# Six attention heads for all tokens at once and two by token halves, with the queries and keys of the two kept on chip between the halves

## The chip, the cores and the metric

The kernel runs on one core of one Trainium2 chip. The metric is the device time of one execution, in microseconds (us). A core has a matrix engine (TensorE, PE in the profile, with PEld for its weight loads), a vector engine (VectorE, DVE), an activation engine (ScalarE, ACT), GpSimd (POOL) and SyncE (SP). Here SP issues most DMAs and POOL issues a few; all of them work side by side and wait for each other only where a semaphore says so. Each engine takes its own instructions in a fixed order.

## The reference, cut to what matters

The model has an mLSTM layer and then a differential attention layer, each followed by a squared-ReLU MLP; 1024 tokens, width 1024. The change touches only the attention: 8 heads, each with two score maps of width 64 and values of width 128, causal, in query blocks of 128 tokens.

```python
for blk in range(S // Q_BLOCK):
    q0 = blk * Q_BLOCK
    kv_len = q0 + Q_BLOCK
    ...
    p1 = jax.nn.softmax(jnp.where(mask, s1, -jnp.inf), axis=-1)
    p2 = jax.nn.softmax(jnp.where(mask, s2, -jnp.inf), axis=-1)
    a = (p1 - lam * p2).astype(v.dtype)
    outs.append(jnp.einsum('bhqk,bhkv->bhqv', a, v[:, :, :kv_len]))
o = jnp.concatenate(outs, axis=2)
o = rms_norm(o, subln_g, SUBLN_EPS) * (1 - lam_init)
return o.transpose(0, 2, 1, 3).reshape(B, S, B_HEADS * B_V_DIM) @ w_out
```

## The kernel before, in words

Tokens are handled in two halves of 512. Queries (`qdr`), keys (`kdr`) and values (`vdr`) are written to DRAM by the projections and loaded head by head for the attention. A number is kept as a high and a low part, so a product of two such numbers is three matmuls (L189 to L191, and L265 to L267 for the value projection).

A **unit** is one head and one query block, (h, qb); it has n = qb + 1 key blocks. In the order of the program it consists of

- `scores` (L971): for each of the two maps f, matmuls of the query block with the keys' two parts `ka` and `kb` (L985, L986) and a diagonal mask (L987) into PSUM; DVE takes the maximum (L989, L991), ACT the exponential and its sum (L995). There are two PSUM buffers for this, so a map's matmuls wait until ACT has read the map before the last.
- `combine` (L999): DVE joins the two maps (L1006), PE transposes the result block by block (L1012), ACT copies it out (L1013).
- `values` (L1016): n products with the head's values `v` (L1026), a copy and a sum of squares on ACT (L1027, L1029).
- after four units of one head, `subnorm` (L1033): four transposes (L1041) and a scaling that gives the operands `yh` and `yl` of the output projection for that head and half. If the place in `yh` and `yl` is still read by the value projection, the result goes to DRAM through POOL (`odr`, L1051) and comes back later by `reload` (L1053, L1056, POOL too); otherwise it is written in place (`direct`, L1043 and L1044).

`load` (L950) fetches a head's queries and keys for the tokens of one job, `load_v` (L967) its values. Both allocate from a pool with two buffers for each name, so a load waits until the head before the last has been read. All their DMAs stand on SP's queue.

Two other pieces of PE work are laid between the units. `chunks` (L1058) is the rest of the value projection: 24 steps of 24 matmuls each, called **fills** here, numbers 4 to 24 within the loop (steps 1 to 3 are ahead of it). Fills 17 to 24 make the values of heads 6 and 7, token block by token block; every second fill stores to `vdr` through ACT and POOL (L902, L905). `project_a` (L1075) is the output projection for the first token half: 8 steps of 24 matmuls of 512 columns, which read the residual `xs` and a weight tile `w_do`. After the loop the same projection for the second half follows (`gemm` at L1172, the same lines L189 to L191).

The loop over the units (L1126) sets the order: in step i it emits the fills that are due, loads, the scores of unit i + 2, combine of unit i, a subnorm, values of unit i - 1, and from a certain point a step of `project_a`. `jobs` (L1099) lists the heads: the first `FULL` of them with all 8 query blocks, then the rest with blocks 0 to 3 and after that once more with blocks 4 to 7. `project_a` begins one step after the last head's subnorm of the first half.

```python
for j, (h, q0, q1) in enumerate(jobs[1:]):
    ln = jobs[j][2] - jobs[j][1]
    load_at[n + 1] = (h, q0, q1)
    v_at[n + ln - 2] = (h, q0, q1)
    if h >= 2 and due[-1][1] < (h // 2 - 1) * NC + q1:
        due.append((n + ln - 2, (h // 2 - 1) * NC + q1))
    n += ln
```

From what the loop emits a scheduler makes the final order of each engine when the program is built; that order is shown below where it matters.

Of the kernel before, what the change touches and what calls it, by code (L numbers as in the profile page):

```python
# [9 lines left out]
F32R = mybir.dt.float32r  # L10
# [7 lines left out]
P = 128  # L18
T = 1024
# [6 lines left out]
BH, BD, BV = 8, 64, 128  # L26
# [2 lines left out]
FFG = (FN,) * FG  # L29
PSEQ = ((0, 1), (0, 2), (0, 5), (0, 6), (1, 1), (0, 7), (1, 5), (0, 3), (1, 6), (0, 4), (1, 2), (2, 1), (1, 7), (2, 5),  # L30
        (1, 3), (2, 6), (1, 4), (2, 2), (3, 1), (2, 7), (3, 5), (2, 3), (3, 6), (2, 4), (3, 2), (3, 7), (3, 3), (3, 4))
AHEAD, LAG, FULL, FILL0 = 2, 2, 5, 3
CUT = 256
LSZ = (2, 2, 1, 3)
QKORD = (2, 3, 4, 5, 0, 1, 6, 7)
# [20 lines left out]
def tile_yoco(ctx: ExitStack, tc: tile.TileContext, x, c, pos, cst, vec, bg, lp, ada,  # L56
              w_in, w_v0, w_v, w_o, w_mo, w_kv, w_vb, w_q, w_do, w_up, w_dn, out):
    nc = tc.nc
    pe, act, dve, sp = nc.tensor, nc.scalar, nc.vector, nc.sync
# [15 lines left out]
    def f32(ap):  # L75
        return ap.bitcast(F32)
# [20 lines left out]
    kdr = dr.tile([2, 2 * BH, BD, T], F32, tag="kdr", name="kdr")  # L97
    qdr = dr.tile([2 * BH, 2, BD, T], F32, tag="qdr", name="qdr")
# [113 lines left out]
    def gemm(srcs, nk, ah, al, consume, nbg=1, halves=(0, 1), first=2, hooks=None,  # L212
# [6 lines left out]
        def load(g):  # L219
            return [srcs[i] if isinstance(srcs[i], tuple) else  # L220
                    wload(srcs[i], [P, nk, P], nbg, hpool=pool if i >= early else None) for i in g]

        nxt = load(groups[0])
        for gi, g in enumerate(groups):
            ws, n = nxt, len(g)
# [13 lines left out]
            for pi, cells in enumerate(passes):  # L239
                for c in cells:  # L240
                    held[c] = cut1(gps(), c[0])
                for k in range(nk):
                    for h, i in cells:
                        mm3(held[h, i], ws[i][0][:, k], ws[i][1][:, k], ah(h, k), al(h, k), k == 0, k == nk - 1)
                    if k == 0 and pi == 0 and gi + 1 < len(groups):
                        nxt = load(groups[gi + 1])
                for h in halves:
                    if joint == gi and (h, 0) in held and (h, 1) not in held:
                        continue
                    idx = sorted(i for hh, i in held if hh == h)  # L250
                    if idx:
                        consume(g[idx[0]], h, [held.pop((h, i)) for i in idx])
                        if after and idx[-1] == n - 1 and (gi, h) in after:
                            after[gi, h]()
# [185 lines left out]
    with ExitStack() as ph:  # L440
# [16 lines left out]
        def small(name):  # L457
            return mp.tile([P, NC, AH], F32, tag=name, name=name)
# [15 lines left out]
        m, fp, nb0, fe, ml, u, mm, b0, me, wsx, wold, em = [  # L474
            small(n) for n in ("m", "fp", "nb0", "fe", "ml", "u", "mm", "b0", "me", "wsx", "wold", "em")]
# [466 lines left out]
    with ExitStack() as ph:  # L942
        kp = ph.enter_context(tc.tile_pool(name="kp", bufs=2))
# [4 lines left out]
        heads, units, lead = {}, {}, [None]  # L948

        def load(h, b0, b1):  # L950
            ka, kb, qs = [], [], []
            qt, kt = slice(b0 * P, b1 * P), slice(0, b1 * P)
            for f in range(2):
                g = 2 * h + f
                a = kp.tile([P, T], F32R, tag=f"ka{f}", name="ka")
                b = kp.tile([P, T], F32R, tag=f"kb{f}", name="kb")
                q = kp.tile([P, T], F32R, tag=f"q{f}", name="q")
                sp.dma_start(out=f32(q[:, qt]), in_=qdr[g, :, :, qt].rearrange("s d t -> (s d) t"))
                for s, t in ((0, a), (1, b)):
                    for dup in range(2):  # L960
                        sp.dma_start(out=f32(t[dup * BD:dup * BD + BD, kt]), in_=kdr[s, g, :, kt])
                ka.append(a)
                kb.append(b)
                qs.append(q)
            heads[h] = dict(ka=ka, kb=kb, qs=qs)

        def load_v(h, b0, b1):  # L967
            heads[h]["v"] = kp.tile([P, NC, BV], F32, tag="v", name="v")
# [148 lines left out]
        norms, back, begun, ahead, steps = [], ([], []), [], [], []  # L1117
        fill, proj, done = chunks(), project_a(), FILL0
        load(*jobs[0])
        load_v(*jobs[0])  # L1120
        for _ in range(done):
# [4 lines left out]
        for i in range(len(seq) + 2 + LAG):  # L1126
# [20 lines left out]
            while norms and norms[0][0] < i - LAG:  # L1147
                h, half = norms[0][1:3]
# [6 lines left out]
            if 0 < i <= len(seq):  # L1155
                h, qb = seq[i - 1]
# [139 lines left out]
```

## Time and profile before

| what | value |
|---|---|
| time, median of 3 runs | 2408.21 us (2405.18 to 2410.25) |
| the profiled execution's own time | 2406.43 us |
| its span, first to last instruction | 2404.7 us |
| lowest of the three runs | 2405.18 us |
| DVE busy | 1555.4 us (65%) |
| ACT busy | 985.1 us (41%) |
| HBM read and written over the span | 110 GB/s |

Times inside the profile are counted from the start of the span. The attention stage lies between about 1324 and 1666 us. "Idle before" in a timeline row is how long that engine stood still ahead of the row, and what released it. The trace shows two matmuls for each value product of one block (576 for the 288 of the program), so a value product of 4 blocks shows as x8 there and as x4 in the order.

### The profile page before, as it was taken

What the parts mean: (1) busy time and instruction counts of PE and PEld (TensorE: products, weight loads), DVE (VectorE), ACT (ScalarE), POOL (GpSimd) and SP (SyncE); (2) the same over time, 40 slices, a digit from 0 to 9 for tenths busy, and PEclk for the clock granted to TensorE, in tenths of its full rate; (3) what the DMA queues carried; (4) which work ended last, traced back from release to release, by engine and by line L of the source; (5) the groups of instructions that cost most, each with busy time, mean ns of one, the idle gap of its engine ahead of it and who ended that gap; (6) DMA issues with size and microseconds to landing.
All of it is one profiled execution on the core that took longest, in us unless ns stands there. A gap on an engine that the chain in (4) does not pass through costs nothing.

```text
span 2404.7 us, 30832 instructions
## 1 busy us (share of the span) xinstructions
PE 2354.6 (98%) x12020; PEld 1977.5 (82%) x12020; DVE 1555.4 (65%) x2559; ACT 985.1 (41%) x1882; POOL 39.1 (2%) x76
## 2 busy tenths in 40 slices
PE   7999999999999999999999999999999999999997
PEld 4899998778888888878788899888878888888886
DVE  7426544787877777777563377675676567566666
ACT  4324633444234323424332477764433333432332
POOL 0000000000000000000000011110000000000000
PEclk9999999999999999999999999999999999999999
DMA  7312142313423432442644654674121111111122
GB/s 309 121 56 85 68 161 79 116 51 123 140 77 90 141 111 65 127 153 79 203 134 149 203 167 154 209 212 167 57 66 35 53 62 44 40 62 57 36 96 79
DMA packets 105757, 266.80 MB, mean 111 GB/s; under 512 B 11786, under 2 KB 43018, under 8 KB 103820
## 3 DMA queue, kind: packets, MB, share of 16 engines
q1 hardware_dynamic: 100876, 250.16, 32.1%
q0 software_dynamic: 4736, 14.68, 1.9%
q8 instruction: 94, 1.54, 0.3%
q14 instruction: 51, 0.42, 0.1%
HBM read 228.03 MB, written 36.77 MB: 110 GB/s over the span
## 4 chain that ended last, share of the span: by engine, by line
PE 80%; DMA 5%; DVE 2%; ACT 1%; issue 0%; SPq 0%; DVEq 0%; ACTq 0%
PE gps L189 23%; PE gps L191 23%; PE gps L190 23%; PE gps L1026 2%; PE gps L265 2%; PE gps L267 2%; PE gps L266 2%; PE sc L985 1%; PE sc L986 1%; PE tps L1012 1%; DMA kb<-kdr 1%; DMA wraw<-in_w_do_dram 1%; DMA ka<-kdr 1%; DMA wraw<-in_w_vb_dram 1%; DVE x L691 0%
## 5 line engine op out<-in xcount | busy, mean ns | idle before, releaser
L189 PE MATMUL gps<-yh,wh 128*128 128x512 f32 x1664 | 655.1, 398 | 4.6 <-DVE yl L1044 2.4
L190 PE MATMUL gps<-yl,wh 128*128 128x512 f32 x1664 | 657.8, 396 | 1.1 <-DVE yl L318 1.1
L191 PE MATMUL gps<-yh,wl 128*128 128x512 f32 x1664 | 655.1, 395 | 0.5 <-DVE wl L172 0.5
L189 PEld LDWEIGHTS gps<-yh,wh 128*128 128x128 f32 x1664 | 312.4, 188 | 82.9 <-DVE yl L1044 2.6
L190 PEld LDWEIGHTS gps<-yl,wh 128*128 128x128 f32 x1664 | 312.6, 188 | 77.2 <-issue 1.7
L191 PEld LDWEIGHTS gps<-yh,wl 128*128 128x128 f32 x1664 | 312.6, 188 | 77.1 <-DVE wl L172 0.9
L171 ACT CAST wh<-wraw 128x1024 fp32r<-128x1024 f32 (+1 forms) x152 | 159.3, 1049 | 407.0 <-DMA wraw<-in_w_up_dram 213.3
L691 DVE SCALAR_TENSOR_TENSOR x<-gps,mod,x 128x512 f32<-128x512 f32 x392 | 286.0, 745 | 48.5 <-PE gps L191 47.0
L172 DVE TENSOR_TENSOR wl<-wraw,wh 128x1024 fp32r<-128x1024 f32 (+1 forms) x152 | 185.9, 1223 | 181.6 <-ACT wh L171 133.9
L265 PE MATMUL gps<-wh,yh 128*128 128x256 f32 (+1 forms) x768 | 223.7, 291 | 5.0 <-ACT sv L902 3.6
L266 PE MATMUL gps<-wl,yh 128*128 128x256 f32 (+1 forms) x768 | 219.9, 286 | 0.0
L267 PE MATMUL gps<-wh,yl 128*128 128x256 f32 (+1 forms) x768 | 219.0, 285 | 0.0
L171 ACT CAST eh<-e 128x1024 fp32r<-128x1024 f32 x56 | 58.7, 1049 | 242.7 <-DVE e L672 242.7
L151 DVE CUSTOM_DVE_ANT_0 adar<-adar,sil 128x1024 f32<-128x1024 f32 x96 | 116.8, 1222 | 53.6 <-DMA adar<-in_ada_dram 52.9
L265 PEld LDWEIGHTS gps<-wh,yh 128*128 128x128 f32 x768 | 145.7, 190 | 6.8 <-ACT sv L902 3.9
L266 PEld LDWEIGHTS gps<-wl,yh 128*128 128x128 f32 x768 | 145.8, 190 | 1.0
L267 PEld LDWEIGHTS gps<-wh,yl 128*128 128x128 f32 x768 | 145.7, 190 | 0.7
L629 ACT ACTIVATE b<-gps 128x512 f32<-128x512 f32 x112 | 66.8, 597 | 177.3 <-PE gps L191 172.1
L995 ACT ACTIVATE pf<-sc,mx 128x256 f32<-128x256 f32 (+7 forms) x128 | 95.1, 749 | 18.7 <-DVE mx L989 12.1
L172 DVE TENSOR_TENSOR el<-e,eh 128x1024 fp32r<-128x1024 f32 x56 | 68.3, 1220 | 46.6 <-PE gps L190 44.4
L189 PE MATMUL gps<-th,lh 128*128 128x512 f32 x224 | 89.1, 398 | 0.5 <-DVE x L691 0.5
L191 PE MATMUL gps<-bh,el 128*128 128x512 f32 x224 | 88.3, 394 | 0.7 <-DVE el L172 0.7
(266 smaller groups left out, 3877.2 us busy)
## 6 DMA issues: line engine op xcount, KB each, us to landing
adar<-in_ada_dram SPq DMA_DIRECT2D x112, 512.0 KB, 4.2
wraw<-in_w_up_dram SPq DMA_DIRECT2D x72, 512.0 KB, 3.4
e<-in_w_dn_dram SPq DMA_DIRECT2D x56, 256.0 KB, 3.1
m<-in_w_dn_dram SPq DMA_DIRECT2D x56, 256.0 KB, 3.1
x<-in_x_dram SPq DMA_DIRECT2D x8, 1024.0 KB, 8.3
wraw<-in_w_mo_dram SPq DMA_DIRECT2D x16, 512.0 KB, 3.3
ka<-kdr SPq DMA_DIRECT2D x32, 256.0 KB, 8.9
kb<-kdr SPq DMA_DIRECT2D x32, 256.0 KB, 9.6
```

Of the source, the lines that this page charges most:

```text
L151: dve.tensor_tensor_reduce(r, r, sil, 1.0, 0.0, ALU.mult, ALU.add, mod[:, n:n + 1])
L171: act.copy(out=ph, in_=src)
L172: dve.tensor_tensor(out=pl, in0=src, in1=f32(ph), op=ALU.subtract)
L189: pe.matmul(ps, lhsT=wh, rhs=a, start=first, stop=False, skip_group_check=more)
L190: pe.matmul(ps, lhsT=wh, rhs=b, start=False, stop=False, skip_group_check=more)
L191: pe.matmul(ps, lhsT=wl, rhs=a, start=False, stop=last, skip_group_check=more)
L265: pe.matmul(ps, lhsT=a, rhs=wh[:, k % 4], start=k == 0, stop=False)
L266: pe.matmul(ps, lhsT=a, rhs=wl[:, k % 4], start=False, stop=False)
L267: pe.matmul(ps, lhsT=b, rhs=wh[:, k % 4], start=False, stop=k == NB - 1)
L629: act.activation(dst, ps, AF.Relu)
L691: dve.scalar_tensor_tensor(xs, ps, mcol(l, 5, nb), xs, ALU.mult, ALU.add)
L995: act.activation(pf[f][:, 0:n * P], pp[f][:, 0:n * P], AF.Exp, bias=mx[:, f:f + 1], accum_out=ls[:, f, qb % 4:qb % 4 + 1])
```

## The change

`FULL` goes from 5 to 6: heads 0 to 5 are done with all tokens in one go, heads 6 and 7 by halves. `load` no longer fetches a part for each half: at a head's first half it allocates the tiles for all tokens, fetches the first half's columns and behind them the second half's; at the second half it does nothing. The values are still loaded once for each half.

```diff
-AHEAD, LAG, FULL, FILL0 = 2, 2, 5, 3
+AHEAD, LAG, FULL, FILL0 = 2, 2, 6, 3
...
         def load(h, b0, b1):
-            ka, kb, qs = [], [], []
-            qt, kt = slice(b0 * P, b1 * P), slice(0, b1 * P)
-            for f in range(2):
-                g = 2 * h + f
-                a = kp.tile([P, T], F32R, tag=f"ka{f}", name="ka")
-                b = kp.tile([P, T], F32R, tag=f"kb{f}", name="kb")
-                q = kp.tile([P, T], F32R, tag=f"q{f}", name="q")
-                sp.dma_start(out=f32(q[:, qt]), in_=qdr[g, :, :, qt].rearrange("s d t -> (s d) t"))
-                for s, t in ((0, a), (1, b)):
-                    for dup in range(2):
-                        sp.dma_start(out=f32(t[dup * BD:dup * BD + BD, kt]), in_=kdr[s, g, :, kt])
-                ka.append(a)
-                kb.append(b)
-                qs.append(q)
-            heads[h] = dict(ka=ka, kb=kb, qs=qs)
+            if b0:
+                return
+            heads[h] = H = {key: [kp.tile([P, T], F32R, tag=f"{tag}{f}", name=tag) for f in range(2)]
+                            for key, tag in (("qs", "q"), ("ka", "ka"), ("kb", "kb"))}
+            for c0, c1 in ((0, b1 * P), (b1 * P, T)):
+                for f in range(2 if c1 > c0 else 0):
+                    g = 2 * h + f
+                    sp.dma_start(out=f32(H["qs"][f][:, c0:c1]),
+                                 in_=qdr[g, :, :, c0:c1].rearrange("s d t -> (s d) t"))
+                    for s, key in enumerate(("ka", "kb")):
+                        for dup in range(2):
+                            sp.dma_start(out=f32(H[key][f][dup * BD:dup * BD + BD, c0:c1]), in_=kdr[s, g, :, c0:c1])
```

In the changed file every line behind `load` stands 3 lines higher, so its L1023 is the L1026 of before. The order of all engines is the same up to about fill 17 and again from the second-half projection on. Three places differ in a way that the prediction speaks of.

**SP's queue, loads of a late head.** Before, the second load of head 5 (numbers of the key tiles: `ka_13434`, `kb_13435` for map 0, `ka_13442`, `kb_13443` for map 1), with the first-half values of heads 6 and 7 (`v_13098`, `v_13294`) in its midst:

```order
L961 DMA ka_13434<-kdr_81 64x1024
L958 DMA q_13436<-qdr_82 128x512
L969 DMA v_13098<-vdr_85 128x512
L961 DMA ka_13434<-kdr_81 64x1024
L961 DMA kb_13435<-kdr_81 64x1024
L969 DMA v_13294<-vdr_85 128x512
L961 DMA kb_13435<-kdr_81 64x1024
L958 DMA q_13444<-qdr_82 128x512
L961 DMA ka_13442<-kdr_81 64x1024 x2
L961 DMA kb_13443<-kdr_81 64x1024 x2
```

Now, the first-half load of head 7 (`ka_13462` and so on), with the first-half values of head 6 (`v_13289`) in its midst and the second half's columns of map 0 behind it:

```order
L962 DMA ka_13462<-kdr_81 64x512
L958 DMA q_13460<-qdr_82 128x512
L962 DMA ka_13462<-kdr_81 64x512
L962 DMA kb_13464<-kdr_81 64x512
L966 DMA v_13289<-vdr_85 128x512
L962 DMA kb_13464<-kdr_81 64x512
L958 DMA q_13461<-qdr_82 128x512
L962 DMA ka_13463<-kdr_81 64x512 x2
L962 DMA kb_13465<-kdr_81 64x512 x2
L958 DMA q_13460<-qdr_82 128x512
```

The full-width key loads that stood here are gone; half-width ones of the last head stand in their place.

**PE, the values of head 6, second half.** Its value tile is `v_13731` before and `v_13745` now; it holds what the last fill, number 24, has made. Before, its first use stands 86 rows behind the last matmul of fill 24:

```order
L189 MATMUL gps_13903<-yh_75,wh_13895 128x512
L190 MATMUL gps_13903<-yl_76,wh_13895 128x512
L191 MATMUL gps_13903<-yh_75,wl_13896 128x512
L1012 MATMUL tps_13977<-cs_70,pf_13798 128x128 x4
L985 MATMUL sc_13954<-ka_13640,q_13642 128x512
L986 MATMUL sc_13954<-kb_13641,q_13642 128x512
L985 MATMUL sc_13954<-ka_13640,q_13642 128x512
L986 MATMUL sc_13954<-kb_13641,q_13642 128x512
L987 MATMUL sc_13954<-negr_9122,identr_9121 128x128
L1012 MATMUL tps_13983<-cs_70,pf_13798 128x128 x2
L1026 MATMUL gps_13989<-v_13731,at_13873 128x128 x2
```

Now it stands 23 rows behind it. Ahead of the rows shown and behind fill 24 there are only 2 value products, the scores of one unit with 4 transposes between its maps, and 3 value products:

```order
L1038 MATMUL rps_13828<-cs_70,o32_13508 128x128 x4
L1009 MATMUL tps_13868<-cs_70,pf_13765 128x128 x4
L1023 MATMUL gps_13877<-v_13543,at_13810 128x128 x4
L1009 MATMUL tps_13874<-cs_70,pf_13765 128x128
L982 MATMUL sc_13845<-ka_13000,q_12998 128x512
L983 MATMUL sc_13845<-kb_13002,q_12998 128x512
L982 MATMUL sc_13845<-ka_13000,q_12998 128x384
L983 MATMUL sc_13845<-kb_13002,q_12998 128x384
L984 MATMUL sc_13845<-negr_9122,identr_9121 128x128
L1023 MATMUL gps_13923<-v_13745,at_13867 128x128 x4
```

The second half of head 5 and the first steps of `project_a`, which stood between, have moved: the former ahead of fill 24, the latter behind.

**PE, the end of the stage.** Before, the last subnorm's transposes (`rps_14556`) stand behind the last step of `project_a`, directly ahead of the second-half projection (`gps_14598`):

```order
L189 MATMUL gps_14515<-yh_75,wh_14437 128x512
L190 MATMUL gps_14515<-yl_76,wh_14437 128x512
L191 MATMUL gps_14515<-yh_75,wl_14438 128x512
L1041 MATMUL rps_14556<-cs_70,o32_14344 128x128 x4
L189 MATMUL gps_14598<-yh_75,wh_14588 128x512
L190 MATMUL gps_14598<-yl_76,wh_14588 128x512
L191 MATMUL gps_14598<-yh_75,wl_14589 128x512
```

Now (`rps_14500`) they stand ahead of the last two steps of `project_a` (`gps_14455` is the seventh of eight):

```order
L189 MATMUL gps_14419<-yh_75,wh_14397 128x512
L190 MATMUL gps_14419<-yl_76,wh_14397 128x512
L191 MATMUL gps_14419<-yh_75,wl_14398 128x512
L1038 MATMUL rps_14500<-cs_70,o32_14168 128x128 x4
L189 MATMUL gps_14455<-yh_75,wh_14435 128x512
L190 MATMUL gps_14455<-yl_76,wh_14435 128x512
L191 MATMUL gps_14455<-yh_75,wl_14436 128x512
```

So 48 matmuls of 512 columns lie between the last subnorm and the first use of its result.

The second-half subnorm of head 5 now comes while the value projection still reads its place, so it is no longer `direct`: one more pair of stores and one more pair of reloads stand on POOL's queue (12 reloads behind fill 24, where there were 10).

## The prediction

> **What bounds the kernel now.** I read the page first: TensorE is busy nearly throughout.
>
> ```profile
> span 2404.7 us, 30832 instructions
> PE 2354.6 (98%) x12020; PEld 1977.5 (82%) x12020; DVE 1555.4 (65%) x2559; ACT 985.1 (41%) x1882; POOL 39.1 (2%) x76
> ```
>
> The change adds and removes no matmul: it reorders those of the attention stage from about 1500 to 1666 us and fetches less. So it can only win what PE stands idle there, and what it runs at a lower clock. The busy time in stretches of 20 us (one of 40), second view, shows that (columns: length, PE, PEld, DVE, ACT, POOL, granted PE clock, DMA share, GB/s):
>
> ```profile
> 1480.00:1520.00 40.00, 40.00 (x316) 38.50 (x316) 30.34 (x64) 31.84 (x101) 4.31 (x8) 1.00 0.49 153
> 1540.00:1560.00 20.00, 17.61 (x139) 16.47 (x137) 11.19 (x32) 13.41 (x57) 3.31 (x7) 1.00 1.03 310
> 1560.00:1580.00 20.00, 17.83 (x119) 16.54 (x120) 15.16 (x26) 12.49 (x33) 3.58 (x7) 0.91 0.95 242
> 1580.00:1600.00 20.00, 20.00 (x136) 18.11 (x135) 15.79 (x26) 12.85 (x34) 2.91 (x6) 1.00 1.02 269
> 1600.00:1620.00 20.00, 18.82 (x105) 15.79 (x103) 11.10 (x19) 11.32 (x25) 0.00 (x0) 1.00 0.43 152
> 1660.00:1680.00 20.00, 17.61 (x77) 13.71 (x76) 6.74 (x9) 5.15 (x8) 0.00 (x0) 1.00 0.68 261
> ```
>
> PE is full up to 1540. Then 2.39 + 2.17 + 1.18 + 2.39 = 8.1 us are idle, and 0.09 x 20 = 1.8 us are lost to the clock: 9.9 us, 0.4% of the time, is the most that any reordering here can win. In the same stretch the DMA engines are full (share 0.95 to 1.03 from 1540 to 1600). The third view, PE's timeline, says what it waited for:
>
> ```profile
> 1544.79 0.46 PE L1026 MATMUL gps<-v,at 128*128 128x128 f32 x2 [1.51 <-DMA v<-vdr]
> 1554.48 0.47 PE L986 MATMUL sc<-kb,q 128*128 128x512 f32 x1 [0.45 <-DMA kb<-kdr]
> 1561.71 0.47 PE L986 MATMUL sc<-kb,q 128*128 128x512 f32 x1 [2.15 <-DMA kb<-kdr]
> 1607.83 0.50 PE L985 MATMUL sc<-ka,q 128*128 128x512 f32 x1 [0.54 <-ACT pf L995]
> 1611.39 0.49 PE L189 MATMUL gps<-yh,wh 128*128 128x512 f32 x1 [0.64 <-DVE xs L1089]
> 1666.34 0.50 PE L189 MATMUL gps<-yh,wh 128*128 128x512 f32 x1 [2.39 <-DVE yl L1044]
> 1666.68 0.39 PE L190 MATMUL gps<-yl,wh 128*128 128x512 f32 x1
> 1666.91 0.39 PE L191 MATMUL gps<-yh,wl 128*128 128x512 f32 x1
> ```
>
> In turn: head 6's first-half values; twice the second keys of head 5, loaded a second time; two short waits around `project_a`; and the last subnorm, directly ahead of the second-half projection, whose matmuls then start 0.23 us apart. Finer windows show the clock behind two of these waits:
>
> ```profile
> 1560.00:1564.00 4.00, 2.29 (x11) 2.27 (x12) 1.29 (x2) 0.00 (x0) 0.00 (x0) 0.76 1.05 274
> 1564.00:1568.00 4.00, 4.00 (x27) 3.71 (x25) 2.12 (x5) 3.31 (x9) 0.00 (x0) 0.81 1.03 227
> 1664.00:1668.00 4.00, 1.66 (x7) 1.39 (x8) 2.79 (x4) 1.47 (x3) 0.00 (x0) 1.00 1.02 398
> ```
>
> After the 2.15 us wait the clock lost 0.24 x 4 + 0.19 x 4 = 1.7 us; after the 2.39 us wait it lost nothing.
>
> **The change part by part.** *What goes.* Head 5 is loaded once, heads 6 and 7 no longer fetch their first keys again; the two key waits end with that: 0.45 + 2.15 + 1.7 = 4.3 us. The wait for head 6's first-half values goes too: behind fill 20, which makes them, now stand the scores of (5,7), a whole fill and the scores of three small units, more than the 9.3 us of PE work that lay there before (from the fill's end at 1533.97, quoted below, to the wait's begin at 1544.79 - 1.51): 1.5 us. At the end, 48 matmuls at 0.23 us, 11 us, now lie between the last subnorm and its use, so its 2.4 us go. Together 8.2 us. The two short waits (1.2 us) I leave in: ACT and DVE still prepare the weights there. If the work that now covers these places runs out, each returns at its own price.
>
> *What is new at head 7.* Its keys can be fetched only when the scores of (5,7) have freed the buffers, and until its first scores PE has 21 value blocks, 16 transposes, a subnorm, a fill and eight maps with 20 key blocks: by the durations worked out below 4.3 + 1.6 + 0.45 + 24 x 0.115 (half the columns of a 0.23 us matmul) + 20 x 0.14, about 12 us. In these SP's queue must bring 1.5 MB (eight transfers of 128 KB for the keys, two of 256 KB for the queries), beside the reloads of the first half on POOL's queue. Before, the second keys of head 5 came under the same reloads and were late by 0.45 and 2.15 us with 2.5 MB. Bounds: nothing, and all of the 4.3 us again. The smaller transfer is nearer to nothing: 0.8 us.
>
> *The wait that is added.* Head 6's second-half values hold what fill 24 makes. From a fill's last matmul the way is: ACT copies, POOL stores, SP waits for the store and issues the load, the load lands. Fill 20 and fill 24 show it (the DMA rows are the landing times of the transfers issued at 1537.21, at 1539.01 and at 1493.36, from the view of DMAs):
>
> ```profile
> 1533.69 0.28 PE L267 MATMUL gps<-wh,yl 128*128 128x256 f32 x1
> 1534.68 1.07 POOL L905 DMA_DIRECT2D vdr<-sv  x2 [5.19 <-ACT sv L902]
> 1537.21 0.37 SPq L969 DMA_DIRECT2D v<-vdr  x1
> v<-vdr SPq DMA_DIRECT2D x1, 256.0 KB, 7.4
> v<-vdr SPq DMA_DIRECT2D x1, 256.0 KB, 14.1
> v<-vdr SPq DMA_DIRECT2D x1, 512.0 KB, 4.2
> 1575.44 0.28 PE L267 MATMUL gps<-wh,yl 128*128 128x256 f32 x1
> 1576.42 1.07 POOL L905 DMA_DIRECT2D vdr<-sv  x2 [23.21 <-ACT sv L902]
> 1580.38 0.33 SPq L969 DMA_DIRECT2D v<-vdr  x1
> ```
>
> From the end of the fill to the load's issue it took 1537.21 - 1533.97 = 3.2 us and 1580.38 - 1575.72 = 4.7 us; I take 4.0. The landing took 4.2 us with quiet DMA engines, 7.4 and 14.1 us amid the reloads. In the new order two weight tiles (1 MB) stand ahead of it on SP's queue and 12 reloads run on POOL's, but no keys: 7.4, the middle row. So the values are there 11.4 us after fill 24 (7.4 to 18.8). What PE has to do until then, by start times:
>
> ```profile
> 1583.04 0.48 PE L985 MATMUL sc<-ka,q 128*128 128x512 f32 x1
> 1583.88 1.05 PE L1012 MATMUL tps<-cs,pf 128*128 128x128 f32 x8
> 1584.69 0.47 PE L985 MATMUL sc<-ka,q 128*128 128x512 f32 x1
> 1585.53 0.62 PE L1041 MATMUL rps<-cs,o 128*128 128x128 f32 x4
> 1585.98 1.06 PE L1026 MATMUL gps<-v,at 128*128 128x128 f32 x8
> 1586.80 0.48 PE L189 MATMUL gps<-yh,wh 128*128 128x512 f32 x1
> 1589.99 0.47 PE L985 MATMUL sc<-ka,q 128*128 128x512 f32 x1
> 1590.95 0.43 PE L1026 MATMUL gps<-v,at 128*128 128x128 f32 x2
> ```
>
> One map of 6 key blocks is 0.84 us, so 0.14 a block, one of 7 blocks 0.96, a transpose 0.10, a value block 0.82 / 4 = 0.205, a subnorm's transposes 0.45. The 23 rows hold 2 + 3 + 4 value blocks (1.85), two maps of 6 (1.68), one of 7 (0.96), 9 transposes (0.9) and one subnorm (0.45): 5.9 us. PE then waits 11.4 - 5.9 = 5.5 us (1.5 to 12.9). PE takes its rows in order, so all that is queued behind waits too: the second map of that unit, and with it DVE's maximum and ACT's exponential. A wait this long I charge the clock loss of the 2.15 us row, 1.7 us (0 to 1.7).
>
> The Trainium skill, TensorE: Matmul & The Clock Gate, Part 1, says that the clock falls to half after an idle window of about 3.4 us and rises after as long a busy one. By that the new wait costs half of 3.4 us, an estimate of 1.7 too, but the 2.15 us wait should not have lowered the clock, and the gain would be 1.7 us smaller; the row of 1560 to 1564 (0.76) speaks against it.
>
> *No fill behind it.* Between fill 24 and `project_a` stand the scores of five large units with no other PE work; before, a fill or a step of `project_a` stood between such units. The only such stretch of before is head 0's, where ACT and DVE set the pace:
>
> ```profile
> 1364.00:1368.00 4.00, 3.34 (x24) 2.80 (x23) 3.80 (x9) 4.00 (x15) 0.00 (x0) 1.00 0.02 4
> 1368.00:1372.00 4.00, 3.63 (x29) 3.32 (x28) 2.88 (x6) 3.61 (x12) 0.00 (x0) 1.00 0.00 0
> 1372.00:1376.00 4.00, 3.97 (x29) 3.56 (x28) 3.90 (x8) 3.57 (x12) 0.00 (x0) 1.00 0.00 0
> 1376.00:1380.00 4.00, 3.79 (x26) 3.25 (x25) 3.71 (x9) 3.52 (x9) 0.00 (x0) 1.00 0.48 147
> ```
>
> PE is idle 16 - 14.73 = 1.3 us in 16. The new stretch behind the wait has 18 value blocks, 21 transposes and six maps with 39 blocks, 3.7 + 2.1 + 5.5 = 11 us: 1.0 us (0, if ACT works ahead during the wait, to 2.0). Elsewhere the fills lie further apart but one still stands in every long unit pair: nothing, covered by PE's own work as from 1480 to 1520. The extra stores and reloads of head 5 on POOL are needed only by the second-half projection, about 90 us behind fill 24 (1575.72 to 1666.34): nothing.
>
> *The sum.* -8.2 + 0.8 + 5.5 + 1.7 + 1.0 = +0.8 us. Against the profiled execution's 2406.43 us that is 2407.2; that execution lies 1.8 us below the median of 2408.21, so on the scale of the medians I forecast 2409.0 us. With a landing of 5.5 to 9.5 us it is 2407 to 2411.
>
> **The rivals.** About 0.2%, 4.8 us, is what a measurement of this kernel can tell from no change.
>
> *Slower: the values come amid the reloads.* If the load lands as the one of 14.1 us did, the wait is 12.9 us, the sum +8.2, the time 2416.4. It decides from +4.8 on, a wait of 9.5 us, which is a landing of 9.5 + 5.9 - 4.0 = 11.4 us. For it: 12 reloads are issued within the same microseconds, as 10 were at 1536. Against: the keys that shared the engines then are absent. The Trainium skill, DMA: Bandwidth & Descriptors, Issuing engines are not separate DMA queues, says that DMAs of SP and POOL run on the same 16 engines and interleave; the 14.1 us row agrees.
>
> *Faster: the values come quickly.* With 3.2 + 4.2 us the wait is 1.5 us and, as after the 1.51 us wait, costs no clock; head 7's keys are in time, the two short waits (1.2 us) vanish. -8.2 - 1.2 + 1.5 + 1.0 = -6.9: 2401.3. For it: less is fetched, for each of the last three heads 3 MB of queries and keys instead of 1.5 + 2.5. Against: the reloads.
>
> *The saving is moved, not made.* Head 7's first keys wait as head 5's second did, 4.3 us instead of 0.8: +4.3, 2412.5. For it: same reloads, same distance. Against: 1.5 MB, not 2.5.
>
> **How the numbers follow.** Forecast 0.47, slower rival 0.20, faster rival 0.20, moved saving 0.13. Forecast and moved saving are within 0.2%: 0.60. The range reaches nearly to both outer cases: 2401.5 to 2415.5. All bounds at once (-8 and +13 us) lie outside it and count among the 2 in 10.
>
> **What would show it.** Right: no wait for `kb` of more than 1 us; none for `yl` ahead of the second-half projection; one PE row L1023 (`gps` from `v`) behind the last L267 with some 5.5 us idle, released by the DMA of `v`, and a granted clock of about 0.8 in the 4 us behind it. Wrong: that row without a wait, a wait of 10 us there, or idle time spread over L982 rows released by ACT, which would mean that the missing fills cost more than the values.

## The result, and the profile after

The changed kernel is slower. Its median is 2422.68 us (2420.33 to 2424.35, 6 runs) against 2407.07 us of before (2405.18 to 2410.25, 6 runs, the same chip): a ratio of 1.0064, 95% interval 1.0054 to 1.0075, or 15.6 us. The forecast was 2409.0 us in a range that ended at 2415.5. Its profiled execution took 2422.82 us. The page's head:

```profile
span 2421.1 us, 30800 instructions
PE 2362.9 (98%) x12020; PEld 1981.9 (82%) x12020; DVE 1556.3 (64%) x2559; ACT 987.9 (41%) x1882; POOL 41.4 (2%) x80
```

The matmuls are as many as before, yet PE is busy 8.3 us longer (2362.9 against 2354.6): at half clock the eight value rows at 1596.64 below are busy for 2.08 us, eight at full clock in the prediction for 1.06. Of these, 2.5 us lie ahead of the attention stage. The span grew by 16.4 us. The value projection's first matmul of the stage starts 1.7 us later (1325.30 us, before 1323.61), ahead of anything that the change moves; in the runs below it starts between 1322.78 and 1325.83. The other 14.7 us arise between there and the first microseconds of the second-half projection. PE's timeline of after names the waits (L1023 is the L1026 of before, L982 the L985, L1086 the L1089):

```profile
1325.30 0.28 PE L265 MATMUL gps<-wh,yh 128*128 128x256 f32 x1
...
1501.59 0.50 PE L982 MATMUL sc<-ka,q 128*128 128x512 f32 x1 [2.24 <-ACT pf L992]
1523.35 0.33 PE L982 MATMUL sc<-ka,q 128*128 128x128 f32 x1 [0.62 <-ACT pf L992]
1566.79 0.30 PE L982 MATMUL sc<-ka,q 128*128 128x128 f32 x1 [0.46 <-DMA ka<-kdr]
1567.95 0.30 PE L983 MATMUL sc<-kb,q 128*128 128x128 f32 x1 [0.86 <-DMA kb<-kdr]
1591.56 0.33 PE L1009 MATMUL tps<-cs,pf 128*128 128x128 f32 x1 [0.89 <-ACT at L1010]
1592.46 0.50 PE L982 MATMUL sc<-ka,q 128*128 128x512 f32 x1 [0.56 <-ACT pf L992]
1596.64 2.08 PE L1023 MATMUL gps<-v,at 128*128 128x128 f32 x8 [3.02 <-DMA v<-vdr]
1608.35 0.50 PE L982 MATMUL sc<-ka,q 128*128 128x512 f32 x1 [1.19 <-ACT pf L992]
1669.47 0.49 PE L189 MATMUL gps<-yh,wh 128*128 128x512 f32 x1 [1.09 <-DVE xs L1086]
1681.05 0.77 PE L189 MATMUL gps<-yh,wh 128*128 128x512 f32 x1 [5.72 <-DVE xs L1086]
```

These are 16.7 us of idle time where before had 7.7 in the six rows that the prediction shows. They lie, but for one row of 0.62 us, in five places: near 1500 (a unit's exponentials are late, 2.2 us), at 1567 (head 7's keys, 1.3), at 1592 to 1597 (head 6's second-half values and two short waits ahead of them, 4.5), at 1608 (units without a fill, 1.2), and at the end of the stage (6.8). The last row is the first matmul of the second-half projection; it waited for `project_a`'s eighth step, not for `yl`.

The clock is the other part. Stretches of after that are cut where the clock changes (the columns are those of the windows in the prediction: length, PE busy and so on, the granted clock is the third number from the end):

```profile
1499.98:1503.40 3.42, 1.63 (x10) 1.30 (x10) 1.67 (x4) 3.42 (x13) 0.54 (x1) 1.00 0.70 242
1503.40:1506.82 3.42, 3.42 (x14) 2.95 (x14) 2.84 (x7) 3.15 (x15) 0.54 (x1) 0.50 0.40 155
...
1592.15:1595.56 3.41, 1.16 (x5) 0.85 (x5) 2.07 (x5) 2.54 (x9) 2.03 (x4) 1.00 1.02 407
1595.56:1598.97 3.41, 2.33 (x10) 2.24 (x11) 0.36 (x1) 0.41 (x3) 0.55 (x1) 0.50 1.03 396
1598.97:1602.39 3.42, 3.42 (x12) 2.94 (x11) 1.16 (x2) 1.51 (x6) 0.00 (x0) 0.50 0.85 321
...
1674.06:1677.48 3.42, 1.27 (x6) 0.69 (x4) 1.21 (x2) 0.63 (x1) 0.00 (x0) 1.00 0.70 210
1677.48:1680.89 3.41, 0.00 (x0) 0.00 (x0) 1.89 (x2) 1.06 (x2) 0.00 (x0) 0.50 0.28 97
1680.89:1684.31 3.42, 3.26 (x8) 2.62 (x9) 0.69 (x1) 0.61 (x1) 0.00 (x0) 0.50 0.83 234
```

Half of the busy time in the rows at 0.50 is lost: 1.7 us behind the place at 1500, 1.2 + 1.7 = 2.9 behind the values, 1.6 at the end, 6.2 us in all against 1.7 before. Idle time and clock together: (16.7 - 7.7) + (6.2 - 1.7) = 13.5 of the 14.7 us. All idle time of PE between the two starts grew by 9.3 us (23.2 against 13.9), so most of the other 1.2 us is not in waits, and where it lies stays open.

Two places are not in the prediction. Near 1500 the releaser is ACT, so ACT's own timeline and SP's queue say why it was late:

```profile
1490.34 0.82 SPq L176 DMA_DIRECT2D wraw<-in_w_do_dram  x2
```

```profile
1499.36 1.04 ACT L171 CAST wh<-wraw 128x1024 fp32r<-128x1024 f32 x1 [3.44 <-DMA wraw<-in_w_do_dram]
1500.31 0.58 ACT L992 ACTIVATE pf<-sc,mx 128x384 f32<-128x384 f32 x1
```

The cast makes the weights of `project_a`'s second step, which are used more than 100 us later; the scheduler has put it here, ahead of a unit's exponentials. Its tile was asked for at 1490.34, behind ten key and query transfers of head 5 that are now full-width, and was there 9.0 us later. ACT stood still for 3.44 us and the exponentials with it. Before, the same cast waited 0.84 us and no PE row shows it.

The end of the stage is read from DVE's rows that finish a step of `project_a`, steps 5 to 8 (with the sum over step 7's square, L1093, among them), and from SP's queue:

```profile
1661.34 0.75 DVE L1086 SCALAR_TENSOR_TENSOR xs<-gps,mod,xs 128x512 f32<-128x512 f32 x1 [6.92 <-DMA xs<-xdr]
1668.67 0.74 DVE L1086 SCALAR_TENSOR_TENSOR xs<-gps,mod,xs 128x512 f32<-128x512 f32 x1
1673.83 0.74 DVE L1086 SCALAR_TENSOR_TENSOR xs<-gps,mod,xs 128x512 f32<-128x512 f32 x1
1675.32 0.69 DVE L1093 TENSOR_TENSOR acc<-acc,xq 128x512 f32<-128x512 f32 x1 [0.75 <-ACT xq L1092]
1680.04 0.75 DVE L1086 SCALAR_TENSOR_TENSOR xs<-gps,mod,xs 128x512 f32<-128x512 f32 x1
```

```profile
1651.23 0.92 SPq L337 DMA_DIRECT2D x<-xdr  x2
...
1676.04 0.32 SPq L1080 DMA_DIRECT2D xs<-xdr  x1
```

A step's 24 matmuls take 5.6 us. Step 8's were done at 1681.05 - 5.72 = 1675.33, but its residual tile was asked for only at 1676.04. `project_a` has two buffers for two kinds of tile, the residual `xs` and its square `xq`, which ACT makes and DVE adds up. Step 8's tile goes where step 7's square was, and the fetch was issued when the sum over that square had ended (1675.32 + 0.69 = 1676.01). The tile was added at 1680.04, and only that released the next projection. Step 5's tile was late as well: it came behind two transfers of 1 MB for the next projection.

### The profile page after: what moved, and what is told of

Same layout as the page of the kernel before. It is cut to its first block, busy times and chain, and to the rows that moved or that the text cites. A ratio compares the mean times of both kernels' runs of the same rounds, so it can differ in the third digit from the quotient of the medians.

```text
span 2421.1 us, 30800 instructions
## 1 busy us (share of the span) xinstructions
PE 2362.9 (98%) x12020; PEld 1981.9 (82%) x12020; DVE 1556.3 (64%) x2559; ACT 987.9 (41%) x1882; POOL 41.4 (2%) x80
## 4 chain that ended last, share of the span: by engine, by line
PE 80%; DMA 4%; DVE 2%; ACT 1%; issue 0%; SPq 0%; DVEq 0%; ACTq 0%
PE gps L189 23%; PE gps L191 23%; PE gps L190 23%; PE gps L1023 2%; PE gps L265 2%; PE gps L266 2%; PE gps L267 2%; PE sc L982 1%; PE sc L983 1%; PE tps L1009 1%; DMA wraw<-in_w_vb_dram 1%; DMA kb<-kdr 1%; DMA wraw<-in_w_do_dram 1%; DMA ka<-kdr 1%; DVE x L691 0%
## 5 line engine op out<-in xcount | busy, mean ns | idle before, releaser
L992 ACT ACTIVATE pf<-sc,mx 128x128 f32<-128x128 f32 (+7 forms) x128 | 95.2, 749 | 22.5 <-DVE mx L986 13.0
```

The costliest lines, as they stand in the source:

```text
L992: act.activation(pf[f][:, 0:n * P], pp[f][:, 0:n * P], AF.Exp, bias=mx[:, f:f + 1], accum_out=ls[:, f, qb % 4:qb % 4 + 1])
```

## The experiments

Theory A, as first put after the two traces: the loss is in the new order of the stage, at separate places. Rivals: B, the kept load itself; and, for each place, that the wait would only move. For the end of the stage the runs later needed two theories of their own, C (the 1 MB transfers) and D (the shared buffers). Each kernel ran in five rounds beside the kernel before; a difference in us is against the median of before from the same session (2405.74 us for runs 1 to 4, 2407.92 for 5 to 8, 2406.14 for 9 to 12) unless said otherwise.

**1. The change without its load.** `FULL` is 6, `load` is that of before.

```diff
-AHEAD, LAG, FULL, FILL0 = 2, 2, 5, 3
+AHEAD, LAG, FULL, FILL0 = 2, 2, 6, 3
```

> Six heads for all tokens and two by halves, but with the load of before: heads 6 and 7 fetch their first keys a second time, nothing is kept. Theory A: the loss of 15.6 us comes from the new order of the stage (the last three steps of project_a back to back, head 6's values behind a late last fill, a weight cast that blocks ACT behind a full-width key load) and not from the kept keys; then this kernel shows the same waits and takes 2420 to 2428 us, the change's time or a little more, since 2 x 2.5 MB are fetched where the change fetches 2 x 1.5 MB. Theory B: the kept load itself (40 half-width transfers issued in a row on SP's queue) costs most of it; then this kernel takes 2407 to 2412 us. PE waits of over 5 us ahead of the second-half projection speak for A.

Measured: 2428.24 us, ratio 1.0087 (1.0073 to 1.0101), 22.5 us slower than before. PE and ACT at the longest wait, and the end:

```profile
1602.97 0.79 PE L985 MATMUL sc<-ka,q 128*128 128x512 f32 x1 [9.82 <-ACT pf L995]
...
1687.21 0.76 PE L189 MATMUL gps<-yh,wh 128*128 128x512 f32 x1 [6.44 <-DVE xs L1089]
```

```profile
1600.49 1.04 ACT L171 CAST wh<-wraw 128x1024 fp32r<-128x1024 f32 x1 [8.52 <-DMA wraw<-in_w_do_dram]
```

B falls: without the kept keys the same order loses as much (by the medians more; the two intervals just touch). What the second fetch costs here is mostly a place in a queue: a weight tile stands behind the key transfers on SP's queue, and its cast blocks ACT for 8.52 us. The end waits as in the change.

**2. The last fills earlier.**

```diff
+        due[-1] = (due[-1][0] - 3, due[-1][1])
+
         def goal(i):
```

> The change with its last fills due three steps earlier, so that fill 24 stands 12 small score maps and two large ones ahead of head 6's second-half values. Theory A (the values wait is a matter of where fill 24 stands): the 3.02 us wait for v, the clock loss of 3.4 us between 1592 and 1604 and the two ACT waits ahead of it (0.89 and 0.56) go, some 1 to 2 us come back because five large units now have no fill between them: 2415 to 2419 us. Rival (the stretch is paced by ACT and DVE whatever the fills do): the idle time only moves to rows of the scores released by ACT, 2420 us or more. The wait of 5.72 us at the end of the stage stays in both.

Measured: 2413.08 us, ratio 1.0030 (1.0019 to 1.0041): 7.3 us slower than before where the change is 15.6 slower. PE's longest rows between 1570 and the end:

```profile
1582.66 0.71 PE L1023 MATMUL gps<-v,at 128*128 128x128 f32 x4 [1.27 <-ACT at L1010]
...
1672.02 0.76 PE L189 MATMUL gps<-yh,wh 128*128 128x512 f32 x1 [6.29 <-DVE xs L1086]
```

No row waits for `v` any more, no clock is lost there, and some 2.8 us in four rows released by ACT are what the stretch without fills costs. The gain of 8.3 us is a little more than A had it (4 to 8): the place's 4.5 + 2.9 us are gone, the keys' 1.3 with them, and the units without fills wait 1.6 us more than the 1.2 of the change, which makes 7.1. The idle time at the end is as it was.

**3. The weight casts late.** A list `exps` collects the exponentials of all units.

```diff
-            nxt = wload(None, [P, NB, P], 0, r=raws[0])
+            with tc.issue_after(exps[-6].ins):
+                nxt = wload(None, [P, NB, P], 0, r=raws[0])
...
-                        nxt = wload(None, [P, NB, P], 0, r=raws[nb + 1])
+                        with tc.issue_after(exps[-6].ins):
+                            nxt = wload(None, [P, NB, P], 0, r=raws[nb + 1])
```

> The change with the weight casts of project_a kept behind a unit's exponentials on ACT's queue that is emitted three units before the step. Theory A: the 3.44 us in which ACT stood still at 1499 for a weight tile, and with it PE's 2.24 us wait and 1.7 us of clock loss, go: 2418 to 2420 us. Rival (the exponentials were late by themselves, the cast only stood where ACT had nothing to do): the PE wait near 1500 stays and the time is 2421 us or more; also possible that project_a's first step then waits for its weights, which would show as a PE wait ahead of the first L189 of the stage.

Measured: 2415.92 us, but with runs from 2412.83 to 2421.40; ratio 1.0042 (1.0027 to 1.0056), which just touches the change's interval. The profiled execution is the longest of the six (span 2419.6). Near 1500 it shows:

```profile
1501.54 0.49 PE L1023 MATMUL gps<-v,at 128*128 128x128 f32 x2 [1.78 <-DMA v<-vdr]
```

The ACT wait is gone, so the cast did block ACT. Behind it stood a second wait: head 4's values, made by fill 16, come late too, and in this execution the clock was lost all the same. What the edit is worth alone, the spread leaves open.

**4. The steps in pairs.**

```diff
-                steps.append(next(proj, None))
+                for _ in range(2 if len(steps) in (1, 4) else 1):
+                    steps.append(next(proj, None))
```

> The change with project_a's second and third step, and its fifth and sixth, emitted in the same step of the loop, so that two of the eight steps are left behind the last values where there were three and a half. Theory A (steps that follow each other without other work are paced by the fetch of the residual and of the weights, about 6.2 us for 5.6 us of matmuls, and the projection behind has to wait for the last of them): of 1.09 + 5.72 us and 1.7 us of clock loss at the end some 2.4 to 3.5 us of idle time are left, as before the change: 2416 to 2419 us. Rival (the wait belongs to the handover between the two projections, wherever the steps stand): it stays at 5 us or more and the time at 2421 us or more.

Measured: 2419.87 us, ratio 1.0059 (1.0045 to 1.0073): not to be told from the change. PE's last wait, DVE's row for step 7, and SP's queue ahead of it:

```profile
1678.98 0.76 PE L189 MATMUL gps<-yh,wh 128*128 128x512 f32 x1 [5.70 <-issue]
```

```profile
1672.94 0.75 DVE L1086 SCALAR_TENSOR_TENSOR xs<-gps,mod,xs 128x512 f32<-128x512 f32 x1 [8.02 <-DMA xs<-xdr]
```

```profile
1661.73 1.40 SPq L337 DMA_DIRECT2D x<-xdr  x3
1663.17 0.75 SPq L1080 DMA_DIRECT2D xs<-xdr  x1
```

Step 8's sum with its residual tile ends 0.1 us ahead of PE's row (at 1678.88), so it is again what PE waited for. A's expectation fails: fewer steps at the end, the same wait. Here step 7's tile comes 9.8 us after its issue, behind 3 MB of `x`, and step 8's is asked for only at 1675.41, when the sum over step 7's square has ended. Hence theories C and D.

**5. The residual stream late** (C).

```diff
-        load_x(xt, xdr)
+        with tc.issue_after(xsd[0].ins):
+            load_x(xt, xdr)
```

`xsd[0]` is the last fetch of `xs`.

> The change with the load of the residual stream for the next projection (four transfers of 1 MB, three of which stood on SP's queue between the fetches of project_a's fifth to seventh step) kept behind project_a's last residual fetch. Theory C (formed after the paired steps moved nothing: 3 MB of that load delay the residual tile of step 5 to 8.6 us, and the steps behind never catch up, so the projection waits for step 8): the 5.72 + 1.09 us and 1.7 us of clock loss shrink to 1.5 to 3 us, 2416 to 2418 us. Rival D (two buffers shared by residual tile and its square: each fetch waits for the store of the step before, 6.2 us for 5.6 us of matmuls): the wait stays at 4 us or more and the time at 2421 us or more. A third case would be that the next projection now waits for the residual stream: a PE wait 5 to 15 us behind its start.

Measured: 2421.89 us, ratio 1.0050 (1.0037 to 1.0062), 14.0 us slower than before, not to be told from the change. DVE's rows for steps 5 to 8 and PE's last wait:

```profile
1661.24 0.75 DVE L1086 SCALAR_TENSOR_TENSOR xs<-gps,mod,xs 128x512 f32<-128x512 f32 x1 [2.36 <-PE gps L191]
...
1667.74 0.75 DVE L1086 SCALAR_TENSOR_TENSOR xs<-gps,mod,xs 128x512 f32<-128x512 f32 x1 [3.82 <-DMA xs<-xdr]
...
1673.91 0.75 DVE L1086 SCALAR_TENSOR_TENSOR xs<-gps,mod,xs 128x512 f32<-128x512 f32 x1 [3.69 <-DMA xs<-xdr]
...
1681.25 0.75 DVE L1086 SCALAR_TENSOR_TENSOR xs<-gps,mod,xs 128x512 f32<-128x512 f32 x1 [4.20 <-DMA xs<-xdr]
```

```profile
1682.11 0.76 PE L189 MATMUL gps<-yh,wh 128*128 128x512 f32 x1 [3.67 <-issue]
```

Step 5 is now in time, and from there a step takes 6.5, 6.2 and 7.3 us (the last beside the stream), each waiting for its tile: the shared buffers alone are slower than 5.6 us of matmuls. Here steps 6 and 8 waited for the store of the step before, step 7 for the sum over a square. C explains why step 5 was late, not the pace. It has a share in the end's wait all the same, which fell from 6.8 to 3.7 us, a little below the 4 us that D had set. The time did not follow in the profiled execution because head 7's keys cost 1.3 us of idle time and 3.0 us of clock more there than in the change.

**6. A ring of its own for the residual tile** (D). The two buffers `sv` are free once the fills are done.

```diff
-                xs = ap_.tile([P, HT], F32, tag="ot", name="xs", bufs=2)
+                xs = ap_.tile([P, 2, 2, BV], F32, tag="sv", name="xs").rearrange("p a b v -> p (a b v)")
```

> The change with project_a's residual tile in buffers of its own (the two that the fills' stores no longer use), so that a fetch no longer waits for the square of the step before; the load of the next projection's residual stream stays where it is, but step 5's tile is now fetched ahead of it. Rival D (the shared two buffers set the pace): the wait of 5.72 us goes, 2415 to 2418 us. Theory C (the 3 MB set it): step 6's tile now comes behind them, so the end improves by 3 us at most, 2419 to 2422 us.

Measured: 2415.07 us (11 runs), ratio 1.0028 (1.0018 to 1.0038): 8.4 us of the 15.6 are gone. DVE's row for step 8 and PE's last wait:

```profile
1670.06 0.75 DVE L1086 SCALAR_TENSOR_TENSOR xs<-gps,mod,xs 128x512 f32<-128x512 f32 x1 [0.38 <-PE gps L191]
```

```profile
1670.91 0.47 PE L189 MATMUL gps<-yh,wh 128*128 128x512 f32 x1 [0.89 <-issue]
```

The last step is now released by its own matmuls. D holds: with the 1 MB transfers still on the queue, the end's waits shrink from 6.8 to 0.9 us and no clock is lost there. A tile can now be asked for earlier: step 5's is issued at 1642.40, ahead of the 1 MB transfers (from 1647.27), where in the change it stood behind two of them. So the ring is enough to take the loss away; with it, the same transfers delay nothing that PE waits for.

**7 and 8. Three edits together, on the change and on before.** The fills three steps earlier ahead of all the heads that need them, the casts of run 3, the stream of run 5.

```diff
-                due.append((n + ln - 2, (h // 2 - 1) * NC + q1))
+                due.append((n + ln - 5, (h // 2 - 1) * NC + q1))
```

> The change with the fills due three steps earlier in front of heads 2, 4 and 6 alike, the weight casts of project_a late, and the residual stream late. If the causes are separate their gains add up: 9.6 for the fills, 2 to 4 for the cast and the values of head 4, 4 to 6 for the end: 2403 to 2407 us, level with before or faster. If they are one and the same slack that moves (DVE and ACT pace the units without fills), less than 12 us come: 2410 us or more.

> The kernel before (five heads at once, three by halves, keys fetched twice) with the same three edits as the kernel sent with it. Its residual stream was late already, and its values wait was 1.5 us, so there is less to repair: 1 to 4 us, 2403 to 2407 us. If head 6 in one go and the kept keys are worth what they removed (two key waits of 4.3 us with the clock loss), this kernel is 3 to 5 us slower than the changed one with the same edits; if it is faster, the split of three heads covers more than the kept keys save.

Measured: the change with them 2402.87 us, ratio 0.9975 (0.9964 to 0.9985), faster than before; its one long wait left is 3.61 us at the end. Before with them 2409.90 us, ratio 1.0006 (0.9996 to 1.0015). That misses the 2403 to 2407 us expected. The comparison of the two is not clean, since on before the late cast meets the second fetch of the keys; ACT and PE there:

```profile
1597.02 1.04 ACT L171 CAST wh<-wraw 128x1024 fp32r<-128x1024 f32 x1 [12.32 <-DMA wraw<-in_w_do_dram]
```

```profile
1600.40 1.11 PE L1012 MATMUL tps<-cs,pf 128*128 128x128 f32 x4 [8.05 <-ACT at L1013]
```

**9 and 10. Fills and ring, with and without the late casts.** Both have the fills of run 7 and the ring of run 6; the first also the casts of run 3.

> The change with the fills due three steps earlier ahead of heads 2, 4 and 6, the weight casts late, and the residual tile in its own ring in place of the late residual stream. From the kernel with the first two and the stream late (2402.9 us), whose last wait of 3.61 us and 1.7 us of clock loss belong to the shared ring if that sets the pace of back-to-back steps: 2397 to 2400 us. If the two repairs of the end are worth the same here: 2402 to 2404 us.

> The same without the late casts: the casts of the first two weight tiles stand again far ahead on ACT's queue. If a cast that waits for its tile behind a full-width key load blocks ACT (the 2.24 to 2.79 us waits near 1500 with the clock loss behind them), this takes 3 to 5 us more than its sister; if the earlier fills have already taken that wait away (the tiles are fetched earlier too), the same within 1 us.

Measured: with the casts 2398.15 us, ratio 0.9967 (0.9955 to 0.9980), 8.0 us faster than before; without 2401.83 us, ratio 0.9980 (0.9971 to 0.9988), 4.3 us faster. The two longest waits that the first has left from 1380 us on:

```profile
1589.26 0.50 PE L982 MATMUL sc<-ka,q 128*128 128x512 f32 x1 [0.81 <-ACT pf L992]
...
1658.94 0.47 PE L189 MATMUL gps<-yh,wh 128*128 128x512 f32 x1 [1.14 <-issue]
```

Its clock stays full from 1380 us through the stage. In the kernel without the late casts no row near 1500 waits longer than 0.5 us either: the earlier fills had fetched the weight tiles earlier too. Why it is 3.7 us slower is then open; its idle rows add up to only 0.7 us more, and the two intervals overlap.

**11. The ring on the kernel before.**

> The kernel before with the residual tile in its own ring and nothing else. There the steps of project_a stand between units, 7 to 10 us apart, so a ring of 6.2 us a step binds nothing: 2406 to 2408 us, within 0.1% of before, against 7.6 us that the same edit brought to the changed kernel. A gain of over 3 us would mean that the ring costs something by itself.

Measured: 2406.40 us, ratio 1.0002 (0.9993 to 1.0010). The last wait is the old one:

```profile
1666.67 0.50 PE L189 MATMUL gps<-yh,wh 128*128 128x512 f32 x1 [2.39 <-DVE yl L1044]
```

The ring is worth nothing where the steps end 7.5 us or more apart, and 8.4 us where the last ones touch. So it was the change that made it a bound.

**12. The second fetch of the keys, all else repaired.** Run 9 with the load of before.

> Six heads at once with the load of before (keys fetched twice) and with earlier fills, late casts and the ring. The distance to the sister with the kept keys is what keeping the keys is worth once nothing else waits: 5 us if its price in the unrepaired pair (2428.2 against 2422.7 us) was its own, 0 to 2 us if the second fetch of the keys hurt only because the values came late behind it.

Measured: 2402.91 us, ratio 0.9990 (0.9981 to 0.9999), 4.8 us more than run 9. Its PE rows that run 9 lacks:

```profile
1585.69 1.35 PE L1026 MATMUL gps<-v,at 128*128 128x128 f32 x10 [1.67 <-DMA v<-vdr]
...
1595.77 0.47 PE L986 MATMUL sc<-kb,q 128*128 128x512 f32 x1 [1.48 <-DMA kb<-kdr]
```

With 1.7 us for one stretch of 3.41 us at half clock behind the second they make 4.85 us: keeping the keys is worth its 4.8 us, once nothing else hides it. The other 3.2 us of run 9's gain are the new order with its repairs. Before was not run with all three of these repairs; those that it was run with (runs 8 and 11) made it no faster.

## Why the prediction was wrong, step by step

*The key waits and the first-half values go* (4.3 + 1.5 us): right. No row waits over 1 us for `kb`, none for head 6's first-half values.

*"At the end, 48 matmuls at 0.23 us, 11 us, now lie between the last subnorm and its use, so its 2.4 us go."* This is the step that failed. The wait for `yl` did go, but the cover was taken as free: the 48 matmuls were counted as work that flows at 0.23 us each, and their own supply was not asked for. Before, every step but the last had value products or scores beside it; now the last four follow each other with only a subnorm's four transposes between, and they are fed through two buffers that also take the square. Where a wait of 2.4 us stood there are 6.8 us of waits and 1.6 us of clock; that the buffers are what makes them is shown by runs 6 and 11. This term alone turns +0.8 into 9.2.

*"Elsewhere ... nothing, covered by PE's own work as from 1480 to 1520."* The second miss, and it lies in that very stretch. The fills were looked at, not the loads. A load is also a length: head 5's now has all tokens at once, a weight tile queues behind it, and ACT behind the tile's cast: 2.2 us and 1.7 us of clock. That the cast blocks ACT, run 3 shows; that the full width of the load makes it late is read from the trace, not tried alone.

*The values wait, 5.5 us and 1.7 of clock:* right in place and in mechanism, with some luck in the sum. The load was issued 4.4 us after the fill's end (taken as 4.0) and landed in about 6.5 (7.4); 3.02 us of wait for the values follow two short ones of 1.45 that ACT released and that the term did not have, and the clock, forecast at about 0.8 over 4 us, stood at 0.50 over 6.8 and lost 2.9. That is 7.4 us against 7.2: a shorter wait and a larger loss of clock offset each other. Run 2, which moved the fill, took away 8.3 us. The slower rival, a landing amid the reloads, did not happen.

*Head 7's keys, 0.8 us; the stretch without fills, 1.0:* measured 1.3 and 1.2.

*The two short waits left in, 1.2 us:* gone; one row of 0.6 us stands in another place.

The sum with what was measured: -8.2 + 1.3 + 7.4 + 1.2 + 3.9 + 8.4 - 0.6 = +13.4 us. So the sums of the terms that the prediction had were right within a microsecond, and the two that it put at a gain or at nothing are 12.3 us. Of the rivals the slower one came nearest in number (2416.4 us), by a landing that did not happen; a saving that is moved is what happened, but it went to `project_a`'s residual tile and not to head 7's keys.

## What to carry to other kernels

Work that is moved to cover a wait needs its own supply: before counting matmuls as cover, ask how long a step takes when its neighbour is another such step, which here is freeing a shared buffer (by a store or by the sum over a square), fetch and add: 6.2 to 7.3 us in run 5, for 5.6 us of matmuls. An instruction that prepares something for much later, and stands in an in-order queue ahead of something urgent, is harmless only while its input is early; a longer load elsewhere can end that. A sound change can lose to what it uncovers: with the fills earlier, the casts later and a ring for the tile, the same edit is 0.33% faster than before, and its own saving of 4.8 us shows.

## What the runs showed of the hardware

The prediction could not say why a wait of 2.15 us had cost clock and one of 2.39 had not. In the attention stage of every run the stretches at half clock last 3.41 us or two or three times that, and within a run they begin at multiples of 3.41 us from each other, so within a run there is a fixed raster. Cut along it, before shows:

```profile
1558.77:1562.19 3.42, 1.27 (x7) 0.79 (x7) 0.49 (x3) 0.76 (x5) 0.00 (x0) 0.99 1.07 229
1562.19:1565.60 3.41, 3.41 (x16) 3.23 (x16) 1.59 (x3) 1.51 (x6) 0.00 (x0) 0.51 1.03 274
...
1664.60:1668.01 3.41, 1.67 (x7) 1.40 (x8) 2.28 (x3) 0.87 (x2) 0.00 (x0) 1.00 1.02 395
1668.01:1671.42 3.41, 3.41 (x16) 2.73 (x16) 0.00 (x0) 0.00 (x0) 0.00 (x0) 1.00 0.60 189
```

The shorter wait lay in one cell and left PE 1.27 us busy in it; the next cell ran at half. The longer one lay across two cells and left 1.67 us in the worse. Over the 14 traces, between 1405 and 1710 us, all 20 cells at full clock in which PE was busy for at most 1.47 us are followed by one at half; all with 2.0 us or more by one at full clock; of the 17 between, 8 by half. So a wait of some 2 us costs another 1.7 or nothing, by where it falls on the raster, which moves from run to run. The Trainium skill, TensorE: Matmul & The Clock Gate, Part 1, speaks of a free-running window of 3413 ns, which these traces show; it lets the clock fall after an idle window, where here one that is half idle was enough (1.63 us busy of 3.42 in the first row of after above).
